# Two blocks on one core: the top-k of the gathered tokens' half first, gathers begun in the routing stage, and the output copies placed behind the last weighted sum

## The chip, the cores and the metric

The kernel runs on one core of one Trainium2 chip. The time is device microseconds of one execution of the whole program; the median of three runs is compared. The names of the engines are those of the profile: PE is TensorE (PEld its weight loads), DVE is VectorE, ACT is ScalarE, POOL is GpSimd, SP is SyncE, whose queue issues most transfers.

## What is computed

Two transformer blocks follow each other on 256 tokens of width 1024. The first mixes three branches (convolution, differential attention, attention to a memory), the second a stick-breaking attention and a recurrence. The change touches only the last part, a feed-forward stage that retrieves single neurons ("experts") by product keys:

```python
def peer_ffn(x, w_query, sub_keys, expert_u, expert_v):
    def chunk(xc):                                   # 128 tokens
        q = jnp.einsum('td,dhk->thk', xc, w_query)   # 8 heads
        q = q.reshape(TOKEN_CHUNK, PEER_HEADS, 2, PEER_HALF)
        s = jnp.einsum('thpk,hpnk->thpn', q, sub_keys)
        top_s, top_i = lax.top_k(s, PEER_TOPK)       # 16 of 128, twice per head
        cand_s = top_s[:, :, 0, :, None] + top_s[:, :, 1, None, :]
        cand_i = top_i[:, :, 0, :, None] * PEER_N_KEYS + top_i[:, :, 1, None, :]
        ...
        best_s, best_pos = lax.top_k(cand_s, PEER_TOPK)   # 16 of 256
        idx = jnp.take_along_axis(cand_i, best_pos, axis=-1)
        g = jax.nn.softmax(best_s, axis=-1)
        u = jnp.take(expert_u, idx, axis=0)          # 16384 experts
        v = jnp.take(expert_v, idx, axis=0)
        act = jax.nn.gelu(jnp.einsum('td,thkd->thk', xc, u))
        return jnp.einsum('thk,thkd->td', (g * act).astype(v.dtype), v)
```

Each token uses 8 heads x 16 = 128 experts.

## The kernel before

The first 160 tokens (`D`) are done densely: all 16384 experts are streamed. `u_pair(i)`, i = 0 to 63, multiplies two weight tiles `w` of 128x1024 (512 KB each) with the tokens and ACT applies the GELU (line 1158) into `ga`; `v_pair(i)` multiplies two tiles of `v` with `ga` and sums into four banks of PSUM, `yT` (line 1169). Between them, `ga` is multiplied by the gates, which are zero for experts that were not chosen: `onehot_group`, called 40 times (20 groups of 8 tokens, two blocks of experts each), builds one-hot matrices on DVE (`toks`, lines 1127 to 1133), multiplies them on PE (line 1136) and multiplies `ga` by the result on DVE (`mul`, line 1147).

The last 96 tokens (`NG`, all in token half t = 1) are done by gathering: for each of 96 index columns `fetch` (line 1178) fetches 128 rows of `u` from HBM into a tile `gat` (512 KB, issued by POOL), `dot` (line 1185) forms the products on DVE, `weights` applies GELU and gate, and then 96 gathers of rows of `v` are summed on DVE by `axpy` (lines 1201 and 1203) into `acc`. `rows_out` folds `acc` over partitions with a matmul (line 1231), ACT copies the result and POOL issues the output transfer (line 1234). Three buffers (`NB`) take gathers until the top-k tiles are freed; then five more (`MORE`) are there.

Ahead of both stands the routing. For each of 8 heads PE makes the query (lines 307 to 309) and the scores (line 1072); `top16` finds 16 of 128 on DVE in a first round (lines 982, 983) and a second (987 to 989); `cands` adds the two lists on POOL (line 998) and takes 16 of 256 with the same five DVE operations. `decode` turns positions into expert numbers `IDX` (lines 1015 to 1030), `gates` does the softmax and transposes `IDX` and gates on PE (lines 1053 to 1055); `rows_index` packs the index of the gathered tokens into `pk` (line 1084) and sends it by six small transfers into `gi` (line 1088), which the gathers read.

All of that waits in a list `bg` and is taken from it a few estimated microseconds at a time between the matmuls (`background(n)`). The final order on each engine is set by a scheduler that plays the program through on modelled times; each engine then works strictly in that order. `tc.issue_after(x)` tells it to put an instruction behind `x`. The steps of the gathers are paced by

```python
            def advance(i):
                box.setdefault("i0", i - 1)
                while box["n"] < (2 * NG + 1) * (i - box["i0"]) / (LAST - box["i0"]):
                    next(steps)
                    box["n"] += 1
```

with i counting the 128 pairs, so that they are spread evenly from the first call to pair 124.

Of the kernel before, what the change touches and what calls it, by code (L numbers as in the profile page):

```python
# [9 lines left out]
F32 = mybir.dt.float32  # L10
# [5 lines left out]
ALU = mybir.AluOpType  # L16
# [3 lines left out]
P = 128  # L20
# [4 lines left out]
D = T - NG  # L25
# [163 lines left out]
def build(tc, xT, memT, vec, con, con0, wcat, rgw, keysT, u, v, urow, vrow, out):  # L189
    nc = tc.nc  # L190
    es = ExitStack()
    with es:
# [26 lines left out]
        state = dict(next=0, hold=())  # L219
# [48 lines left out]
        bg = []  # L268

        def background(n, pin=False, keep=0):  # L270

            with ExitStack() as s:
                if pin:
                    s.enter_context(tc.issue_after(state["sub"].ins))
                while len(bg) > keep and n > 0:
                    c, f = bg.pop(0)
                    n -= c
                    f()
# [3 lines left out]
        def linP(x):  # L282

            ws = block()
            ps = lin_ps[0].tile([P, 2, T], F32, name="lin")[:, :, :x.shape[-1]]
            for a in range(2):
                for c in range(NC):
                    nc.tensor.matmul(ps[:, a], ws[a][:, c * P:(c + 1) * P], x[:, c], start=c == 0, stop=c == 7)  # L288
            ahead()
            return ps  # L290
# [68 lines left out]
        def statp():  # L359
            return cur["ps"].tile([P, 512], F32, name="stat", tag="stat", bufs=1)  # L360

        def attp():
            return cur["ps"].tile([P, 512], F32, name="att", tag="att", bufs=cur.get("natt", 2))
# [4 lines left out]
        def smt(n, w=512, bufs=2, dt=F32):  # L368
            return cur["sm"].tile([P, w], dt, name=n, tag=n, bufs=bufs)
# [94 lines left out]
        with ExitStack() as e1:  # L464
# [6 lines left out]
            def bigt(n, dt=F32):  # L471
# [4 lines left out]
                name=nc.get_next_instruction_name(), act_func_set_id=LN_EXP, ins=[], outs=[]))  # L476
# [125 lines left out]
            for j in range(4):  # L602
# [3 lines left out]
                g = smt("gate", 512, 3).rearrange("p (a b) -> p a b", a=2)  # L606
# [86 lines left out]
            s1, s2 = statp(), attp()  # L693
# [13 lines left out]
            for c in range(NC):  # L707
                t = smt("nrm", T)
# [70 lines left out]
            for j in range(2):  # L779
                ps = linT(h2)  # L780
                nc.vector.tensor_mul(xp[:, 2 * j:2 * j + 2, 3:], ps, bc2(rx))
                for c in (2 * j, 2 * j + 1):
                    nc.vector.tensor_scalar(xc[:, c], xp[:, c, 0:T], V("conv_w_2", c * 4), V("conv_b_2", c),
                                            op0=ALU.mult, op1=ALU.add)
# [135 lines left out]
            for j in range(2):  # L920
                for k, ps in enumerate(linK(mx, 0, None if j else (scp(), scp()))):
                    sl = slice(4 * j + 2 * k, 4 * j + 2 * k + 2)
                    g = smt("gate", 512, 3).rearrange("p (a b) -> p a b", a=2)
# [20 lines left out]
        yT = [yps.tile([P, 2, T], F32, name=f"y{b}") for b in range(4)]  # L944
# [6 lines left out]
        gi = rows.tile([P, 2, NG], F32, name="gi")  # L951
        sG = rows.tile([P, NG], F32, name="sG")
        cG = rows.tile([P, NG], F32, name="cG")
# [5 lines left out]
        with ExitStack() as e3:  # L959
# [5 lines left out]
            tk = e3.enter_context(tc.tile_pool(name="tk", bufs=1, side="right", reuse_waits="tile"))  # L965
# [5 lines left out]
            V16 = tk.tile([P, 2, 8, 2, 16], F32, name="V16")  # L971
            I16 = tk.tile([P, 2, 8, 2, 16], U32, name="I16")
# [5 lines left out]
            def top16(val, idx, src, tag):  # L978
                w = src.shape[-1]

                def f1():
                    nc.vector.max(out=val[:, 0:8], in_=src)
                    nc.vector.max_index(out=idx[:, 0:8], in_max=val[:, 0:8], in_values=src)

                def f2():
                    s2 = tk.tile([P, w], F32, name=tag, tag=tag, bufs=1)
                    nc.vector.match_replace(out=s2, in_to_replace=val[:, 0:8], in_values=src, imm_value=-3.0e38)
                    nc.vector.max(out=val[:, 8:16], in_=s2)
                    nc.vector.max_index(out=idx[:, 8:16], in_max=val[:, 8:16], in_values=s2)  # L989

                c = 0.07 + 0.00104 * w
                bg.append((2 * c, f1))
                bg.append((3 * c, f2))

            def cands(hd, t):
                def f():
                    cs = tk.tile([P, 16, 16], F32, name="cs", bufs=2)
                    nc.gpsimd.tensor_add(cs, V16[:, t, hd, 0].unsqueeze(2).to_broadcast([P, 16, 16]),
                                         V16[:, t, hd, 1].unsqueeze(1).to_broadcast([P, 16, 16]))
                    n = len(bg)  # L1000
                    top16(BS[:, t, hd], BP[:, t, hd], cs.rearrange("p a b -> p (a b)"), "cs2")
                    new = bg[n:]
                    del bg[n:]
                    bg[0:0] = new
                return f
# [27 lines left out]
            box = {}  # L1033

            def logits(t):
                def f():
                    gg_ = (pk[:, 1] if t else tk.tile([P, P], F32, name="gexp", bufs=1)).rearrange(
                        "p (a b) -> p a b", a=8)
                    nc.vector.tensor_sub(gg_, BS[:, t], BS[:, t, :, 0:1].to_broadcast([P, 8, 16]))
                    box[t] = gg_  # L1040
                return f

            def gates(t):
# [18 lines left out]
                    state["dve"] = nc.vector.tensor_copy(gT[:, 1, tl], r0)  # L1062
                return f

            for hd in range(8):
                pq = linT(h3, hd == 0)
                q = tk.tile([P, 2, T], F32, name="q", bufs=1)
                nc.scalar.copy(q, pq)
                pss = gps.tile([P, 512], F32, name="gp", tag="gp").rearrange("p (t h n) -> p t h n", t=2, h=2)
                for t in range(2):  # L1070
                    for p_ in range(2):
                        nc.tensor.matmul(pss[:, t, p_], q[:, p_, t * P:(t + 1) * P], kT[:, 2 * hd + p_],
                                         start=True, stop=True)
                ss = tk.tile([P, 2, 2, P], F32, name="ss", bufs=2)
                nc.scalar.copy(ss, pss)
                for t in range(2):
                    for p_ in range(2):
                        top16(V16[:, t, hd, p_], I16[:, t, hd, p_], ss[:, t, p_], "s2")
                    bg.append((0.0, cands(hd, t)))
                background(2.5)  # L1080
            def rows_index():


                nc.vector.scalar_tensor_tensor(pk[:, 0].bitcast(U32), IDX[:, 1, 0], float(P), IDX[:, 1, 1],
                                               op0=ALU.mult, op1=ALU.add)
                for o_, g, nq in groups:
                    for q_ in range(nq):
                        nc.gpsimd.dma_start(gi[q_ * g:(q_ + 1) * g, :, o_:o_ + g],
                                            pk[P - NG + o_:P - NG + o_ + g, :, q_ * g:(q_ + 1) * g])
# [15 lines left out]

            bg.append((0.1, rows_h))
            for t in (1, 0):
                bg.append((0.1, logits(t)))
                for q_ in range(2):
                    bg.append((4.3, decode(t, q_)))  # L1110
                bg.append((3.0, gates(t)))
                if t:
                    bg.append((0.3, rows_index))
# [39 lines left out]
            def act_of(i):  # L1153
                j = 2 * i
                return ga[0][:, j:j + 2] if j < 64 else ga[1][:, j - 64:j - 62] if j < 96 else ga[2][:, j - 96:j - 94]

            def u_pair(i):
                state["act"] = nc.scalar.activation(act_of(i), linP(h3f[:, :, :D]), AF.Gelu_apprx_tanh)  # L1158
# [38 lines left out]
            def axpy(k, m, g):  # L1197
                with tc.issue_after(state["dve"].ins):
                    if m not in acc:
                        acc[m] = rows.tile([P, 1024], F32, name=f"acc{m}", tag=f"row{m}")  # L1200
                        nc.vector.tensor_scalar_mul(acc[m], g, cG[:, k:k + 1])
                    else:
                        nc.vector.scalar_tensor_tensor(acc[m], g, cG[:, k:k + 1], acc[m], op0=ALU.mult, op1=ALU.add)  # L1203

            def gathered():

# [29 lines left out]
            acc = {}  # L1236
# [4 lines left out]
# [6 lines that stand above are left out]

            i = 0
            while bg:
                u_pair(i)  # L1250
                background(4.6)
                i += 1
# [27 lines left out]
        for b in range(4):  # L1280
            o = ga[0][:, 2 * b:2 * b + 2]
            nc.scalar.copy(o[:, 0], yT[b][:, 0, :D])  # L1282
            nc.vector.tensor_copy(o[:, 1], yT[b][:, 1, :D])  # L1283
            nc.sync.dma_start(yo[:, 2 * b:2 * b + 2], o)


# [20 lines left out]
```

## Time and profile before

| | before |
|---|---|
| median of 3 runs | 1322.68 us (1321.14 to 1325.76) |
| profiled execution, its own time | 1325.82 us |
| its span in the trace | 1324.0 us |
| PE busy | 1250.4 us (94%) |
| DVE busy | 937.6 us (71%) |
| POOL busy | 218.3 us (16%) |
| moved by DMA | 340.75 MB, mean 257 GB/s |
| weight tiles `w` of u and v, 512 KB each | 256 |
| gathers `gat`, 512 KB each | 192 |

Busy times overlap between engines. All rows below are of the profiled execution, with times counted from the start of its span.

### The profile page before, as it was taken

What the parts mean: (1) busy time and instruction counts of PE and PEld (TensorE: products, weight loads), DVE (VectorE), ACT (ScalarE), POOL (GpSimd) and SP (SyncE); (2) the same over time, 40 slices, a digit from 0 to 9 for tenths busy, and PEclk for the clock granted to TensorE, in tenths of its full rate; (3) what the DMA queues carried; (4) which work ended last, traced back from release to release, by engine and by line L of the source; (5) the groups of instructions that cost most, each with busy time, mean ns of one, the idle gap of its engine ahead of it and who ended that gap; (6) DMA issues with size and microseconds to landing.
All of it is one profiled execution on the core that took longest, in us unless ns stands there. A gap on an engine that the chain in (4) does not pass through costs nothing.

```text
span 1324.0 us, 24472 instructions
## 1 busy us (share of the span) xinstructions
PE 1250.4 (94%) x9948; PEld 1211.4 (91%) x9948; DVE 937.6 (71%) x1806; ACT 456.7 (34%) x733; POOL 218.3 (16%) x222
## 2 busy tenths in 40 slices
PE   8999999999999999998999999999999999999902
PEld 7999999899999999887999999999999999999901
DVE  6799888888997687847998544875547865440095
ACT  7546677668647458845313010000100000000000
POOL 0000000000000000000012532323412253330072
PEclk9999999999999999999999999999999999999955
DMA  8555543444565564324676999999999999999384
GB/s 293 191 191 178 164 133 120 131 139 156 161 194 174 177 203 137 124 75 157 207 260 205 410 409 408 409 388 384 379 339 353 366 384 409 409 409 409 142 334 189
DMA packets 94864, 340.75 MB, mean 257 GB/s; under 512 B 10576, under 2 KB 12048, under 8 KB 94624
## 3 DMA queue, kind: packets, MB, share of 16 engines
q1 hardware_dynamic: 66752, 237.98, 50.8%
q0 software_dynamic: 28000, 101.22, 19.9%
q8 instruction: 78, 1.28, 0.4%
q14 instruction: 34, 0.28, 0.1%
HBM read 338.01 MB, written 1.05 MB: 256 GB/s over the span
## 4 chain that ended last, share of the span: by engine, by line
PE 78%; DMA 6%; DVE 6%; issue 5%; ACT 3%; POOL 1%; POOLq 0%; SPq 0%; ACTq 0%
PE lin L288 18%; PE y L1169 15%; PE lin L308 10%; PE lin L307 10%; PE lin L309 10%; DMA w<-in_v 6%; PE gp L1136 1%; PE lin L341 1%; PE lin L343 1%; PE lin L342 1%; POOL gat L1178 1%; PE stat L459 1%; ACT whi L247 1%; DVE I L989 1%; PE sc L840 1%
## 5 line engine op out<-in xcount | busy, mean ns | idle before, releaser
L288 PE MATMUL lin<-h3f,w 128*128 128x160 f32 x2048 | 290.6, 302 | 1.8 <-issue 1.8
L1169 PE MATMUL y<-ga,w 128*128 128x160 f32 x2048 | 287.3, 301 | 1.0 <-issue 0.5
L288 PEld LDWEIGHTS lin<-h3f,w 128*128 128x128 f32 x2048 | 281.3, 191 | 3.0 <-issue 2.8
L1169 PEld LDWEIGHTS y<-ga,w 128*128 128x128 f32 x2048 | 279.4, 190 | 3.5 <-issue 1.8
L248 DVE TENSOR_TENSOR wlo<-raw,whi 128x1024 fp32r<-128x1024 f32 x188 | 229.4, 1223 | 64.3 <-ACT whi L247 63.4
L247 ACT CAST whi<-raw 128x1024 fp32r<-128x1024 f32 x188 | 196.2, 1049 | 167.7 <-PE lin L308 124.9
L308 PE MATMUL lin<-hl,whi 128*128 128x256 f32 x704 | 200.4, 285 | 0.0
L309 PE MATMUL lin<-hh,wlo 128*128 128x256 f32 x704 | 200.0, 284 | 0.0
L307 PE MATMUL lin<-hh,whi 128*128 128x256 f32 x704 | 199.9, 284 | 0.0
L1203 DVE SCALAR_TENSOR_TENSOR acc<-gat,cG,acc 128x1024 f32<-128x1024 f32 x94 | 120.8, 1285 | 55.7 <-DMA gat<-in_vrow,gi 54.1
L1185 DVE CUSTOM_DVE_ANT_0 gat<-gat,hrow 128x1024 f32<-128x1024 f32 x96 | 116.1, 1223 | 33.0 <-DMA gat<-in_urow,gi 32.9
L1178 POOL DMA_INDIRECT gat<-in_urow,gi x96 | 105.3, 1097 | 200.1 <-DVE sG L1185 187.4
L309 PEld LDWEIGHTS lin<-hh,wlo 128*128 128x128 f32 x704 | 132.7, 189 | 2.2 <-issue 1.9
L308 PEld LDWEIGHTS lin<-hl,whi 128*128 128x128 f32 x704 | 132.8, 189 | 1.7 <-issue 1.4
L307 PEld LDWEIGHTS lin<-hh,whi 128*128 128x128 f32 x704 | 132.6, 188 | 1.4 <-issue 1.0
L1178 POOL DMA_INDIRECT gat<-in_vrow,gi x96 | 96.9, 1009 | 181.2 <-DVE acc L1203 71.4
L1158 ACT ACTIVATE ga<-lin 128x320 f32<-128x320 f32 x64 | 28.0, 437 | 243.6 <-PE lin L288 230.5
L535 DVE SCALAR_TENSOR_TENSOR cacc<-ub,VT,cacc 128x256 f32<-128x256 f32 x240 | 103.9, 479 | 0.0
L955 POOL DMA_DIRECT2D fold<-in_con x1 | 0.7, 701 | 595.9 <-DVE gate L924 595.9
L1147 DVE SCALAR_TENSOR_TENSOR ga<-gp,ga 128x256 f32<-128x256 f32 (+1 forms) x60 | 29.1, 511 | 79.3 <-PE gp L1136 54.9
L1282 ACT COPY ga<-y 128x160 f32<-128x160 f32 x4 | 1.2, 292 | 206.9 <-PE y L1169 206.9
L1283 DVE COPY ga<-y 128x160 f32<-128x160 f32 x4 | 1.2, 320 | 68.7 <-ACT ga L1282 68.7
(372 smaller groups left out, 2135.2 us busy)
## 6 DMA issues: line engine op xcount, KB each, us to landing
raw<-in_wcat SPq DMA_DIRECT2D x188, 512.0 KB
w<-in_u SPq DMA_DIRECT2D x128, 512.0 KB
w<-in_v SPq DMA_DIRECT2D x128, 512.0 KB
gat<-in_urow,gi POOLq DMA_INDIRECT x96
gat<-in_vrow,gi POOLq DMA_INDIRECT x96
m_t<-in_memT SPq DMA_DIRECT2D x4, 256.0 KB
xr<-in_xT SPq DMA_DIRECT2D x2, 512.0 KB
kT<-in_keysT SPq DMA_DIRECT2D x1, 1024.0 KB
```

The costliest lines, as they stand in the source:

```text
L247: nc.scalar.copy(h, raw)
L248: state["sub"] = nc.vector.tensor_sub(l, raw, h.bitcast(F32))
L288: nc.tensor.matmul(ps[:, a], ws[a][:, c * P:(c + 1) * P], x[:, c], start=c == 0, stop=c == 7)
L307: nc.tensor.matmul(ps[:, a], wh, ah[:, c], start=(a, c) in first, stop=False)
L308: nc.tensor.matmul(ps[:, a], wh, al[:, c], start=False, stop=False)
L309: nc.tensor.matmul(ps[:, a], wl, ah[:, c], start=False, stop=(a, c) in last)
L535: nc.vector.scalar_tensor_tensor(cacc[:, c], s, w, cacc[:, c], op0=ALU.mult, op1=ALU.add)
L1147: state["dve"] = nc.vector.scalar_tensor_tensor(g_[:, :, tl], p_, 1.0 / GSCALE, g_[:, :, tl], op0=ALU.mult, op1=ALU.mult)
L1169: nc.tensor.matmul(yT[c // 2][:, c % 2, :D], ws[a][:, c * P:(c + 1) * P], g[:, a], start=False, stop=i == 63 and (a, c % 2) == (1, 1))
L1178: nc.gpsimd.indirect_dma_start(g, None, src, bass.IndirectOffsetOnAxis(gi[:, 0, k:k + 1].bitcast(U32), 0))
L1185: nc.vector.tensor_tensor_reduce(out=g, in0=g, in1=h, scale=1.0, scalar=0.0, op0=ALU.mult, op1=ALU.add, accum_out=sG[:, k:k + 1])
L1203: nc.vector.scalar_tensor_tensor(acc[m], g, cG[:, k:k + 1], acc[m], op0=ALU.mult, op1=ALU.add)
```

## The change

Three edits. First, in the loop over heads, the scores of half t = 0 go into a tile `ss0` that keeps all eight heads; only the top-k steps of half t = 1 are put into the list there, and those of t = 0 follow behind the index of the gathered tokens. Second, `rows_index` sets a mark, and from then on the loop of u pairs that works off the routing list calls `advance`, so that gathers may begin there, with the three buffers there are at that time. Third, the DVE copies of `yT` to the output tile are put behind the last `axpy` (`state["sum"]`).

```diff
@@ -1062,6 +1062,7 @@
+            ss0 = tk.tile([P, 8, 2, P], F32, name="ss0")
             for hd in range(8):
                 pq = linT(h3, hd == 0)
                 q = tk.tile([P, 2, T], F32, name="q", bufs=1)
@@ -1071,18 +1072,20 @@
-                ss = tk.tile([P, 2, 2, P], F32, name="ss", bufs=2)
-                nc.scalar.copy(ss, pss)
-                for t in range(2):
-                    for p_ in range(2):
-                        top16(V16[:, t, hd, p_], I16[:, t, hd, p_], ss[:, t, p_], "s2")
-                    bg.append((0.0, cands(hd, t)))
-                background(2.5)
+                ss = tk.tile([P, 2, P], F32, name="ss", bufs=2)
+                nc.scalar.copy(ss, pss[:, 1])
+                nc.scalar.copy(ss0[:, hd], pss[:, 0])
+                for p_ in range(2):
+                    top16(V16[:, 1, hd, p_], I16[:, 1, hd, p_], ss[:, p_], "s2")
+                bg.append((0.0, cands(hd, 1)))
+                background(3.4)
+
             def rows_index():
                 nc.vector.scalar_tensor_tensor(pk[:, 0].bitcast(U32), IDX[:, 1, 0], float(P), IDX[:, 1, 1],
                                                op0=ALU.mult, op1=ALU.add)
+                box["gi"] = True
@@ -1105,6 +1108,11 @@
             for t in (1, 0):
+                if t == 0:
+                    for hd in range(8):
+                        for p_ in range(2):
+                            top16(V16[:, 0, hd, p_], I16[:, 0, hd, p_], ss0[:, hd, p_], "s2")
+                        bg.append((0.0, cands(hd, 0)))
                 bg.append((0.1, logits(t)))
@@ -1200,7 +1208,7 @@
-                        nc.vector.scalar_tensor_tensor(acc[m], g, cG[:, k:k + 1], acc[m], op0=ALU.mult, op1=ALU.add)
+                        state["sum"] = nc.vector.scalar_tensor_tensor(acc[m], g, cG[:, k:k + 1], acc[m], op0=ALU.mult, op1=ALU.add)
@@ -1247,6 +1255,8 @@
             while bg:
+                if "gi" in box:
+                    advance(i)
                 u_pair(i)
                 background(4.6)
@@ -1280,7 +1290,8 @@
             nc.scalar.copy(o[:, 0], yT[b][:, 0, :D])
-            nc.vector.tensor_copy(o[:, 1], yT[b][:, 1, :D])
+            with tc.issue_after(state["sum"].ins):
+                nc.vector.tensor_copy(o[:, 1], yT[b][:, 1, :D])
             nc.sync.dma_start(yo[:, 2 * b:2 * b + 2], o)
```

Where the instructions stand now is shown at three places. The first is the end of DVE's program (`acc<-gat` are the weighted sums of gathered rows, `ga<-y` the copies of the dense output). Before:

```order
L1203 SCALAR_TENSOR_TENSOR acc_11562<-gat_11789,cG,acc_11562 128x1024
L1203 SCALAR_TENSOR_TENSOR acc_11562<-gat,cG,acc_11562 128x1024
L1283 COPY ga_7132<-y_7134 128x160
L1203 SCALAR_TENSOR_TENSOR acc_11562<-gat,cG,acc_11562 128x1024
L1283 COPY ga_7132<-y_7135 128x160
L1203 SCALAR_TENSOR_TENSOR acc_11562<-gat,cG,acc_11562 128x1024
L1283 COPY ga_7132<-y_7136 128x160
L1283 COPY ga_7132<-y_7137 128x160
```

And of the changed kernel, the last rows of DVE's program:

```order
L1211 SCALAR_TENSOR_TENSOR acc_11511<-gat_12329,cG,acc_11511 128x1024
L1211 SCALAR_TENSOR_TENSOR acc_11511<-gat_12352,cG,acc_11511 128x1024
L1211 SCALAR_TENSOR_TENSOR acc_11511<-gat_12375,cG,acc_11511 128x1024
L1211 SCALAR_TENSOR_TENSOR acc_11511<-gat_12378,cG,acc_11511 128x1024
L1294 COPY ga_7132<-y_7134 128x160
L1294 COPY ga_7132<-y_7135 128x160
L1294 COPY ga_7132<-y_7136 128x160
L1294 COPY ga_7132<-y_7137 128x160
```

Before, the first copy had 39 weighted sums behind it; now all four copies follow the last sum.

The second place is POOL's program at the start of the gathers (`cs` are the candidate sums of one head and token half, `gi<-pk` the index transfers, `gat<-in_urow` the gathers). Before:

```order
L998 TENSOR_TENSOR cs<-V_7191 128x256 x16
L1088 DMA gi<-pk 32x2x32 x4
L1088 DMA gi<-pk 64x2x64 x2
L1178 DMA gat<-in_urow,gi 128x1024 x3
L1178 DMA gat_8491<-in_urow,gi 128x1024
```

And in the changed kernel:

```order
L998 TENSOR_TENSOR cs<-V_7191 128x256 x11
L1091 DMA gi<-pk 32x2x32 x4
L1091 DMA gi<-pk 64x2x64 x2
L998 TENSOR_TENSOR cs<-V_7191 128x256 x2
L1186 DMA gat<-in_urow,gi 128x1024 x3
L998 TENSOR_TENSOR cs<-V_7191 128x256 x2
L1186 DMA gat<-in_urow,gi 128x1024 x3
L998 TENSOR_TENSOR cs<-V_7191 128x256
L1186 DMA gat<-in_urow,gi 128x1024 x5
```

The index transfers moved ahead of five of the sixteen candidate sums, and the gathers stand between the last of these.

The third place is DVE's program at the first two dots (ISA rows with `gat`) of the changed kernel; before, no dot stood ahead of the last top-k or decode instruction.

```order
L982 MAX BS<-cs 128x8
L988 MAX V_7191<-s_8318 128x8
L1193 ISA gat,sG<-gat,hrow_7936 128x1024
L1193 ISA sG 128x1
L983 MAX_INDEX BP<-BS,cs 128x8
L987 MATCH_REPLACE cs_8306<-BS,cs 128x256
L989 MAX_INDEX I_7192<-V_7191,s_8318 128x8
L982 MAX BS<-cs 128x8
L1193 ISA gat,sG<-gat,hrow_7936 128x1024
L1193 ISA sG 128x1
```

Eight dots now stand ahead of the end of the decode of t = 0. Of the gathers' 192 dots and sums, 99 stood ahead of the last `mul` of the one-hot groups on DVE, and 104 do now. On PE the transposes of `gates(1)` moved from u pairs 9.9 and 10.9 to 4.4 and 5.9, those of `gates(0)` from 12.2 and 13.3 to 13.4 and 14.7; the matmuls of the one-hot groups keep their places to within 1.5 pairs.

## Rows read from the trace of the kernel before

**Rows 1.** The page: DVE's busy tenths and the transfers, 40 slices of the span.

```profile
DVE  6799888888997687847998544875547865440095
...
GB/s 293 191 191 178 164 133 120 131 139 156 161 194 174 177 203 137 124 75 157 207 260 205 410 409 408 409 388 384 379 339 353 366 384 409 409 409 409 142 334 189
```

**Rows 2.** Stages: length, PE, PEld, DVE, ACT, POOL busy (count), PE clock, DMA share, GB/s.

```profile
662.00:742.00 80.00, 77.06 (x556) 75.79 (x555) 72.46 (x289) 17.96 (x31) 22.96 (x29) 0.98 0.77 263
742.00:1064.00 322.00, 322.00 (x2828) 318.79 (x2827) 202.82 (x401) 22.28 (x55) 102.23 (x95) 1.00 0.99 382
1064.00:1190.00 126.00, 125.47 (x919) 123.60 (x916) 69.59 (x56) 0.00 (x0) 53.00 (x54) 1.00 1.02 406
1190.00:1235.00 45.00, 44.56 (x320) 43.29 (x319) 0.00 (x0) 0.00 (x0) 0.72 (x1) 1.00 1.03 409
1235.00:1258.00 23.00, 23.00 (x172) 23.00 (x171) 0.00 (x0) 0.12 (x1) 0.00 (x0) 1.00 0.06 21
1258.00:1311.00 53.00, 6.41 (x34) 5.61 (x34) 50.86 (x43) 2.10 (x6) 33.34 (x32) 0.59 0.84 322
```

**Rows 3.** Timeline of the end: start, duration, instruction, count, idle before it and its releaser.

```profile
1187.22 0.95 POOL L1178 DMA_INDIRECT gat<-in_vrow,gi  x1 [1.62 <-DVE acc L1203]
1188.22 1.28 DVE L1203 SCALAR_TENSOR_TENSOR acc<-gat,cG,acc 128x1024 f32<-128x1024 f32 x1 [1.26 <-DMA gat<-in_vrow,gi]
1189.77 0.94 POOL L1178 DMA_INDIRECT gat<-in_vrow,gi  x1 [1.60 <-DVE acc L1203]
...
1258.20 0.33 DVE L1283 COPY ga<-y 128x160 f32<-128x160 f32 x1 [68.70 <-ACT ga L1282]
...
1258.56 3.74 SPq L1284 DMA_DIRECT2D out<-ga  x4
...
1259.99 1.98 POOL L1178 DMA_INDIRECT gat<-in_vrow,gi  x1 [69.28 <-DVE ga L1283]
...
1261.53 48.82 DVE L1203 SCALAR_TENSOR_TENSOR acc<-gat,cG,acc 128x1024 f32<-128x1024 f32 x37
...
1310.41 3.68 PE L1231 MATMUL lin<-acc,fold 128*64 128x512 f32 x4 [5.11 <-DVE acc L1203]
```

**Rows 4.** Transfers, 1100 to 1190 us: queue (q0 gathers, q1 weight tiles), packets, MB, share.

```profile
q0 software_dynamic: 5043, 18.36, 51.2%
q1 hardware_dynamic: 5044, 18.34, 51.1%
```

**Rows 5.** The same of 1190 to 1235 us.

```profile
q1 hardware_dynamic: 4076, 14.85, 82.7%
q0 software_dynamic: 972, 3.51, 19.7%
```

**Rows 6.** The same of 1262 to 1306 us, with the mean rate.

```profile
DMA packets 5049, 16.71 MB, mean 380 GB/s; under 512 B 540, under 2 KB 1052, under 8 KB 5048
...
q0 software_dynamic: 4504, 16.37, 95.9%
```

**Rows 7.** Transfers from 1300 to 1324 us, GB/s in slices of 0.6 us.

```profile
GB/s 403 403 410 416 410 403 416 416 403 205 27 0 0 0 0 0 0 0 0 0 0 0 0 0 0 0 55 205 178 0 0 0 0 0 0 0 0 0 0 0
```

**Rows 8.** Timeline: index transfers, the first gather, the first dot.

```profile
715.06 3.35 POOL L1088 DMA_DIRECT2D gi<-pk  x6 [13.04 <-DVE pk L1084]
...
721.77 1.84 POOL L1178 DMA_INDIRECT gat<-in_urow,gi  x1 [3.36 <-DMA gi<-pk]
...
730.20 1.26 DVE L1185 CUSTOM_DVE_ANT_0 gat<-gat,hrow 128x1024 f32<-128x1024 f32 x1 [3.11 <-DMA gat<-in_urow,gi]
```

**Rows 9.** DVE groups, 620 to 735 us: count, busy us, mean ns, idle before.

```profile
L988 DVE MAX8 V<-s 128x8 f32<-128x128 f32 x32 | 8.8, 276 | 0.0
...
L988 DVE MAX8 BS<-cs 128x8 f32<-128x256 f32 x16 | 6.5, 409 | 0.0
```

**Rows 10.** Timeline of the u pairs: PE at the first transpose, PE after the first gathers.

```profile
709.72 0.30 PE L1053 MATMUL gp<-ident,IDX 128*128 128x128 f32 x1 [1.14 <-DVE IDX L1030]
...
735.22 0.57 PEld L288 LDWEIGHTS lin<-h3f,w 128*128 128x128 f32 x4 [0.79 <-issue]
...
738.21 0.44 ACT L1158 ACTIVATE ga<-lin 128x320 f32<-128x320 f32 x1 [9.17 <-remote]
```

**Rows 11.** Timeline of ACT: two u pairs after each other at full pace.

```profile
746.17 0.44 ACT L1158 ACTIVATE ga<-lin 128x320 f32<-128x320 f32 x1 [4.06 <-PE lin L288]
750.52 0.44 ACT L1158 ACTIVATE ga<-lin 128x320 f32<-128x320 f32 x1 [3.91 <-PE lin L288]
```

## The prediction

> **What bounds the kernel now.** I read the page's slices first [rows 1]: up to slice 21 the transfers stay below 300 GB/s, from slice 22 (728 us) they run near 409 GB/s, and in slices 36 to 38 (1191 to 1291 us) DVE falls to nothing and then to 9 and transfers drop to 142 GB/s. Next the stages [rows 2]. From 742 to 1258 us PE is busy without a break at a granted clock of 1.00, so PE sets the pace there; a u pair takes 4.35 us [rows 11], a weight tile half of that, 2.17 us. Transfers run at 382 to 409 GB/s at the same time: there are two limits close together. From 1235 to 1258 us they do almost nothing (21 GB/s), and after 1258 us PE has only 6.41 us of work in 53 while DVE is full: the kernel ends with a tail of gathers alone.
>
> The timeline of the end says why [rows 3]. DVE does a weighted sum at 1188.22 and then sits idle for 68.70 us in front of the copy of `yT`, which needs PE's last matmul. With DVE, the buffers stop: POOL waits 69.28 us before its next gather at 1259.99. So 39 weighted sums and 31 gathers come after PE is done. The reader is to see that this idle time is on no engine's account but that of the order: the sums behind the copy did not need it.
>
> **Output copies behind the last sum.** This removes no work; it lets the gathers run on beside PE's last 70 us. From 1190 us on the trace has these transfers left: 14.85 MB of weight tiles and 3.51 MB of gathers already issued [rows 5], and 16.37 MB of gathers later [rows 6], 34.7 MB in all. At the 409 GB/s that stages with both queues full hold [rows 2, 4] they take 84.9 us, to 1275; in the trace the last gather's bytes landed at 1306 [rows 7]. Gain 31.1 us. If the mixed end ran only at the 380 GB/s of the gathers alone [rows 6], it would be 91.4 us and 24.6. More than 31 it can't be, since 409 is the highest rate any stage shows.
>
> Beside this I check PE. In 1100 to 1190 us both queues moved the same, 18.3 MB each [rows 4], one tile and one gather (0.524 MB each) per 2.56 us, as the gathers at 1187.22 and 1189.77 show [rows 3]. PE wants a tile per 2.17 us and lives off its ring of 13 tiles. The 28.3 tiles left at 1190 (14.85 / 0.524) then land at 1190 + 72.5 = 1262.5 instead of 1235, and PE ends some 4 us after the last, at about 1267 instead of 1258. That costs 9 us of PE and nothing at the end, because the gathers end later.
>
> Last byte to end stays: 1324.0 - 1306 = 18.0 us for the buffered sums, the fold on PE at 1310.41, ACT's copies and the output transfer [rows 3, 7]. New in it are the four copies (0.33 us each, [rows 3]) behind the last sum and SP's four output transfers (3.74 us to issue): about 5 us and their landing, beside the 13.6 us from the last sum (1310.4) to the end. So they cost nothing; without that cover they would cost their 5 us. Nothing else waits behind these copies on DVE.
>
> Here the Trainium skill speaks against the change: "DMA: Bandwidth & Descriptors", section Where 436 GB/s comes from, says that transfers from HBM are bound by about 358 GB/s per core. By that the 34.7 MB would take 97 us and end at 1287, a gain of 19 instead of 31. The trace decides otherwise: 409 GB/s over 45 us [rows 2, 5], so the Trainium skill's limit does not hold in this run.
>
> **Top-k of t = 1 first, gathers in the routing stage.** The index leaves DVE at about 714.6 us: POOL's index transfers start at 715.06 and the first gather at 721.77, waiting for them [rows 8]. In the new order ten second rounds of t = 0 and six of its 256-wide top-16 have moved behind the index: 10 x 3 x 0.276 + 6 x 5 x 0.409 = 20.6 us [rows 9]. They overlap a little, so I take 20: index at 694.5, first gather at about 701.5. The two candidate sums now ahead of it on POOL wait for DVE rows some 6 us behind the index, no longer than the index transfers take (721.77 - 715.06 = 6.7).
>
> What that is worth is not 20 us. With three buffers, and the first dot 14 us behind the index on DVE (eight second rounds and sixteen 256-wide operations, 13.2 us by [rows 9], and a microsecond of gates), gathers trickle. What survives is read from the order: 104 instead of 99 dots and sums stand ahead of the last one-hot `mul`. Between the first one-hot group and that `mul`, gathers are locked to PE's pace through DVE's order, so the lead stays 5 gathers: 2.62 MB or 6.4 us at 409 GB/s. Bounds: 0, if DVE or POOL lose it again; 8 gathers (10 us), if the stage after 1064 us starts with three more already landed.
>
> Eight second copies on ACT (half of the old copy each) cost ACT's start-up only; ACT is busy 17.96 us of 80 there [rows 2]. Nothing is on the path.
>
> **What the early gathers cost PE.** PE works in order, and the transposes of `gates` wait for DVE. Before, PE waited 1.14 us at the first one [rows 10]. It now meets that transpose 5.5 pairs earlier: 708.6 - 5.5 x 4.35 = 684.7 us. DVE's first decode, counted in the same way some 8 us ahead of the index, ends at 686.5: 2 us. The transposes of `gates(0)` come 7.5 pairs after the second of `gates(1)` (694 us), at 727. DVE was through with both halves at 730.20 - 3.11 = 727.1 [rows 8], the first decode of t = 0 some 5 us before. Now seven dots stand ahead of that decode (7 x 1.22 = 8.5 us), and they wait for gathers: the first landed 8.4 us after its issue [rows 8], so at 710, about 3 us after DVE gets there. That gives 722 + 8.5 + 3 = 734 and a wait of 7 us on PE, between 2 (the rows just fit) and 12 (each dot waits). I add 2 us for a lower clock behind so long a gap. Against it, the first eight gathers at once cost PE 9.17 - 4.0 = 5.2 us at 738.21 [rows 10, 11], with three buffers perhaps nothing. Net: 2 + 7 + 2 - 1.1 - 5.2 = +4.7; I take +5, from -5 (no waits) to +15 (long waits, and a burst when five buffers come later). This moves everything behind it, since PE has no idle time to give up until 1258 [rows 2].
>
> **The sum.** Last gather byte: 1306 - 31.1 - 6.4 + 5 = 1273.5; plus 18.0 gives a span of 1291.5, 32.5 us less. The profiled execution's own time is 1325.82, so it would be 1293.3; the median of the runs is 1322.68, and I predict **1290 us**. All low bounds together (31.1 + 10 + 5) give 1277, all high ones (24.6 + 0 - 15) 1313.
>
> **Rivals.** *PE becomes the end.* If the lead is larger and PE loses nothing, gathers end with the weight tiles and the end is PE's: 1267 minus a few us, plus 14 for sums, fold and output: span 1280, **1279 us**. For: PE is unbroken to 1258. Against: the order keeps the lead at 5. Chance 0.16.
>
> *The early start is lost in the routing stage.* DVE's dots wait in order, `gates(0)` comes late, PE stands 12 us or more, or the burst recurs: the first part turns into a loss of 5 to 12 us against a gain of 31. Span 1298 to 1305, **1300 us**. For: three buffers, eight dots ahead of the decode. Against: first landing 8.4 us is short beside the 14 us DVE needs from index to first dot. Chance 0.22.
>
> *The mixed rate does not hold.* With all gathers in flight to the end, transfers fall to the 380 GB/s of [rows 6]: 6.5 us later, 1296 us, and 1303 with no lead. Against: [rows 2, 4, 5]. Chance 0.04. By the limit of the Trainium skill named above, the same sum would give 1301 us.
>
> *Slower than before.* While gathers take half of the transfers, PE is short of tiles from about 1207 us. Should its clock fall to the lower level (1.2 GHz), a tile takes 4.35 instead of 2.56 us, 1.8 us more each; with some 23 tiles left then, PE ends 41 us later, at 1313, and the kernel near **1322**. It decides from 24 tiles on: if the clock falls before 1205 us and stays low, the change loses. Clocks below 1 stand in stages where PE had gaps of microseconds (0.98 in 662 to 742, 0.59 after 1258, [rows 2]); from 1064 to 1190, short gaps for tiles included, it stayed 1.00. The Trainium skill ("TensorE: Matmul & The Clock Gate", section HAM oscillation — how this bites in real kernels) describes such a fall in kernels that wait for data after every few matmuls; no stage here shows it at gaps this short. Chance 0.03.
>
> *No change* would need the order to be without effect; the copies do stand last on DVE. Chance 0.01.
>
> **How the numbers follow.** My forecast, 1284 to 1297 us, holds 0.54. The range reaches to the first two rivals, 1279 to 1302, and leaves out the ends of both, the poor rate's worst and the slow clock: about 2 in 10. A measurement of this kernel can tell 0.3%, 4 us. Faster 0.96, the same 0.02 (no change, and half of the slow-clock rival), slower 0.02.
>
> **What would show it.** Right: no idle of DVE over a few us after 1064 us; transfers at 409 GB/s up to the last gather, at 1268 to 1280; PE's last matmul between 1260 and 1273, with a few tenths of waiting per tile after about 1210; first gather at 701 us; PE waiting at the transpose of `gates(0)` near 727 us. Wrong: a first gather near 721, DVE waits of over 10 us for gathers ahead of t = 0's decode, a clock below 1 between 1200 and 1260, or a gap of over 20 us between the last tile and the last gather.

## The result and the profile after

The changed kernel takes 1291.35 us (median of 3 runs, 1290.32 to 1291.59) where the kernel before takes 1322.68: a ratio of 0.9757, 95% interval 0.9728 to 0.9786. It is faster by 31.3 us. Its profiled execution has a span of 1289.6 us, 34.4 us under that of before, whose profiled execution was itself 3.1 us above its median (1325.82 us).

The page: the same two rows as in [rows 1], 40 slices of a span that is now 1289.6 us.

```profile
DVE  6889988888998777855899864588545886445444
...
GB/s 294 189 194 182 164 138 124 132 116 147 164 200 161 196 202 157 148 67 99 181 235 240 354 409 409 409 408 363 382 383 342 356 360 392 409 409 408 409 409 231
```

DVE no longer falls to 0 and rises to 9 at the end; it keeps a 4 or 5 up to the last slice, and the transfers stay at 408 to 409 GB/s where [rows 1] has the 142.

The stages, in the columns of [rows 2] (the last three in place of its last one, since the end has moved):

```profile
662.00:742.00 80.00, 74.29 (x539) 73.33 (x538) 73.72 (x290) 16.95 (x29) 26.50 (x33) 0.98 0.82 285
742.00:1064.00 322.00, 322.00 (x2817) 318.76 (x2816) 207.50 (x408) 22.39 (x55) 101.07 (x96) 1.00 0.99 382
1064.00:1190.00 126.00, 126.00 (x930) 124.26 (x929) 67.66 (x55) 0.00 (x0) 51.87 (x53) 1.00 1.02 404
1190.00:1235.00 45.00, 43.03 (x292) 39.82 (x291) 21.86 (x18) 0.00 (x0) 16.10 (x17) 1.00 1.03 409
1235.00:1258.00 23.00, 21.05 (x140) 18.88 (x138) 11.55 (x10) 0.00 (x0) 8.52 (x9) 1.00 1.03 409
1258.00:1276.00 18.00, 15.39 (x103) 13.94 (x104) 11.48 (x10) 2.12 (x6) 2.86 (x4) 1.00 0.86 341
1276.00:1290.00 14.00, 3.15 (x16) 1.44 (x13) 2.55 (x6) 1.16 (x2) 1.12 (x2) 0.73 0.29 75
```

From 1190 to 1258 us DVE now works (21.86 and 11.55 us, against 0.00 before), and PE is no longer full: 43.03 of 45 and 21.05 of 23 us. Its clock stays at 1.00 to 1276 us.

The transfers of 1190 to 1235 us, as in [rows 5]:

```profile
DMA packets 5043, 18.39 MB, mean 409 GB/s; under 512 B 560, under 2 KB 560, under 8 KB 5040
...
q1 hardware_dynamic: 2520, 9.18, 51.2%
q0 software_dynamic: 2520, 9.18, 51.0%
```

Both queues move the same 9.18 MB; before, the weight tiles had 14.85 MB of it.

The timeline of the end, which answers to [rows 3]:

```profile
1263.65 0.95 POOL L1186 DMA_INDIRECT gat<-in_vrow,gi  x1 [1.62 <-DVE acc L1211]
1264.65 1.28 DVE L1211 SCALAR_TENSOR_TENSOR acc<-gat,cG,acc 128x1024 f32<-128x1024 f32 x1 [1.27 <-DMA gat<-in_vrow,gi]
1265.73 2.20 PEld L1177 LDWEIGHTS y<-ga,w 128*128 128x128 f32 x16 [0.36 <-DMA w<-in_v]
...
1269.77 7.89 DVE L1211 SCALAR_TENSOR_TENSOR acc<-gat,cG,acc 128x1024 f32<-128x1024 f32 x6 [1.28 <-DMA gat<-in_vrow,gi]
...
1270.83 3.53 PE L1177 MATMUL y<-ga,w 128*128 128x160 f32 x24 [1.18 <-DMA w<-in_v]
...
1277.58 1.01 DVE L1294 COPY ga<-y 128x160 f32<-128x160 f32 x4
...
1277.71 1.93 PE L1239 MATMUL lin<-acc,fold 128*64 128x512 f32 x4 [0.50 <-DVE acc L1211]
1277.92 2.00 SPq L1295 DMA_DIRECT2D out<-ga  x4
...
1280.55 0.58 POOL L1242 DMA_DIRECT2D out<-gat  x1 [4.02 <-ACT gat L1241]
```

The 68.70 us of idle time on DVE and the 69.28 us on POOL [rows 3] are gone. In their place stand waits of 1.27 us for a gather and 0.36 us for a weight tile (on PEld), one of each per 2.56 us. PE's last matmul of `y` ends at 1274.36 us, the last weighted sum at 1277.66, and the copies follow it in 1.01 us.

The first index, gather and dot, which answer to [rows 8]:

```profile
694.26 3.35 POOL L1091 DMA_DIRECT2D gi<-pk  x6 [0.92 <-DVE pk L1086]
...
700.79 1.05 POOL L1186 DMA_INDIRECT gat<-in_urow,gi  x1 [0.29 <-PE lin L288]
...
708.93 1.23 DVE L1193 CUSTOM_DVE_ANT_0 gat<-gat,hrow 128x1024 f32<-128x1024 f32 x1 [1.67 <-DMA gat<-in_urow,gi]
```

PE at the routing, which answers to [rows 10], and the ACT instruction that one of its waits goes back to (`gexp` are the exponentials of the softmax in `gates`):

```profile
686.41 0.33 PE L1053 MATMUL gp<-ident,IDX 128*128 128x128 f32 x1 [0.37 <-DVE IDX L1030]
...
726.39 2.17 PE L288 MATMUL lin<-h3f,w 128*128 128x160 f32 x14 [1.71 <-ACT ga L1166]
731.91 0.33 PE L1053 MATMUL gp<-ident,IDX 128*128 128x128 f32 x1 [3.35 <-DVE IDX L1030]
```

```profile
724.28 0.31 ACT L1048 ACTIVATE gexp<-gexp 128x128 f32<-128x128 f32 x1 [6.51 <-DVE gexp L1039]
```

### The profile page after: what moved, and what is told of

Same layout as the page of the kernel before. It is cut to its first block, busy times and chain, and to the rows that moved or that the text cites. A ratio compares the mean times of both kernels' runs of the same rounds, so it can differ in the third digit from the quotient of the medians.

```text
span 1289.6 us, 24478 instructions
## 1 busy us (share of the span) xinstructions
PE 1253.5 (97%) x9948; PEld 1211.0 (94%) x9948; DVE 937.0 (73%) x1806; ACT 457.3 (35%) x741; POOL 214.6 (17%) x222
## 3 DMA queue, kind: packets, MB, share of 16 engines
q8 instruction: 78, 1.28, 0.4%
## 4 chain that ended last, share of the span: by engine, by line
PE 43%; issue 20%; DMA 16%; DVE 11%; POOL 6%; ACT 3%; POOLq 0%; SPq 0%; DVEq 0%; ACTq 0%
DMA gat<-in_vrow,gi 10%; PE lin L308 10%; PE lin L307 10%; PE lin L309 10%; POOL gat L1186 6%; DMA gat<-in_urow,gi 5%; DVE acc L1211 2%; PE lin L341 1%; DVE gat L1193 1%; PE lin L343 1%; PE lin L342 1%; DVE wlo L248 1%; PE stat L459 1%; ACT whi L247 1%; DVE I L983 1%
## 5 line engine op out<-in xcount | busy, mean ns | idle before, releaser
L1177 PE MATMUL y<-ga,w 128*128 128x160 f32 x2048 | 293.0, 302 | 5.6 <-DMA w<-in_v 2.8
L1177 PEld LDWEIGHTS y<-ga,w 128*128 128x128 f32 x2048 | 279.9, 190 | 13.3 <-DMA w<-in_v 10.4
L1186 POOL DMA_INDIRECT gat<-in_vrow,gi x96 | 93.3, 972 | 162.6 <-DVE acc L1211 127.4
L308 PE MATMUL lin<-h3lo,whi 128*128 128x256 f32 x128 | 37.3, 291 | 2.3 <-DVE h3lo L384 2.3
```

What stands on the lines that cost most here:

```text
L308: nc.tensor.matmul(ps[:, a], wh, al[:, c], start=False, stop=False)
L1177: nc.tensor.matmul(yT[c // 2][:, c % 2, :D], ws[a][:, c * P:(c + 1) * P], g[:, a], start=False, stop=i == 63 and (a, c % 2) == (1, 1))
L1186: nc.gpsimd.indirect_dma_start(g, None, src, bass.IndirectOffsetOnAxis(gi[:, 0, k:k + 1].bitcast(U32), 0))
```

## The experiments

The theory after the result: nearly all of the gain comes from the four copies, and the end is bound by transfers that the two queues share evenly. The rivals: the earlier start brings a good part of it; or PE's late end has another cause than the transfers. Four kernels were timed together with the kernel before (1323.89 us, median of 15 runs), three others later, again with it (1323.36 us, 9 runs). "Lead" is the number of dots and sums that stand ahead of the last one-hot `mul` on DVE.

**Only the copies moved** (the kernel before with the third edit alone; `state["sum"]` is set as in the change):

```diff
...
-            nc.vector.tensor_copy(o[:, 1], yT[b][:, 1, :D])
+            with tc.issue_after(state["sum"].ins):
+                nc.vector.tensor_copy(o[:, 1], yT[b][:, 1, :D])
```

> The kernel before with the third edit alone (copies of yT behind the last weighted sum). Theory A (DVE's place of the copies was the whole cost, the early gathers give back about what they take): 34.7 MB left at 1190 us end at 1275 us, plus 18 us less a few for a full clock: a span of 1290 to 1294, a median of 1289 to 1294 us, within 3 us of the full change. Theory B (the gathers begun 20 us earlier carry a good part of the 31 us): 1303 to 1312 us.

Measured: 1295.27 us (1294.32 to 1298.24), ratio 0.978 (0.9763 to 0.9798), 28.6 us less; the span is 1293.4. The end of its timeline:

```profile
1264.27 3.53 PE L1169 MATMUL y<-ga,w 128*128 128x160 f32 x24 [1.19 <-DMA w<-in_v]
...
1265.30 14.49 DVE L1203 SCALAR_TENSOR_TENSOR acc<-gat,cG,acc 128x1024 f32<-128x1024 f32 x11 [0.33 <-DMA gat<-in_vrow,gi]
...
1279.84 3.67 PE L1231 MATMUL lin<-acc,fold 128*64 128x512 f32 x4 [6.68 <-DVE acc L1203]
```

So this edit alone brings 28.6 of some 31 us; its interval and that of the changed kernel overlap, so what the other two edits add is not shown by these two times. PE's last matmul of `y` ends here at 1267.80, with gathers still coming: the end is the gathers'. The last eleven sums follow each other without a wait: from 1265.30 us on DVE keeps the pace, at 1.3 us a sum.

**The copies on ACT** (the kernel before, with no wait on the sums, and the second copy of each pair moved to ACT):

```diff
-            nc.vector.tensor_copy(o[:, 1], yT[b][:, 1, :D])
+            nc.scalar.copy(o[:, 1], yT[b][:, 1, :D])
```

> The kernel before with both copies of each pair of yT on ACT, none on DVE, and nothing put behind anything. Theory A (a DVE instruction that waits for PE's last matmul held the sums queued behind it): DVE runs through, 1289 to 1295 us, like the third edit alone. Rival (the sums were held by something else that the edit's order also moved, such as the buffers or the gate values): 1318 to 1325 us.

Measured: 1297.22 us (1294.64 to 1299.78), ratio 0.979 (0.9771 to 0.981), 2 us above the range of the theory and 21 us under that of the rival. The cause of the old stall is thus that the copies stood in DVE's order, not when they were done or where their output went. The 2 us are not traced to one cause: in its trace the dense output's transfers run beside the last gathers, and the last five sums wait 0.18 to 0.19 us each for theirs, where the copies alone have no wait.

**Only the early start** (the first two edits, the copies as before):

```diff
-            with tc.issue_after(state["sum"].ins):
-                nc.vector.tensor_copy(o[:, 1], yT[b][:, 1, :D])
+            nc.vector.tensor_copy(o[:, 1], yT[b][:, 1, :D])
```

> The changed kernel without the third edit: top-k order and early gathers alone; the copies then have 35 weighted sums behind them instead of 39. Theory A: DVE stands about 60 us in front of the copy again, four gathers fewer in the tail (4 x 1.32 = 5.3 us), PE's end 4 us later: 1318 to 1323 us. Theory B: 1300 to 1310 us.

Measured: 1321.9 us (11 runs, 1318.41 to 1323.47), ratio 0.9976 (0.9965 to 0.9987): 2 us less. The end of its timeline:

```profile
1260.49 0.32 DVE L1293 COPY ga<-y 128x160 f32<-128x160 f32 x1 [66.98 <-ACT ga L1292]
...
1262.27 1.98 POOL L1186 DMA_INDIRECT gat<-in_vrow,gi  x1 [67.56 <-DVE ga L1293]
```

The stall is nearly as long as before (66.98 against 68.70 us) and ends 2.3 us later, since PE ends later. By the written order 35 instead of 39 sums stand behind the first copy, 4 x 1.3 = 5 us; less the 2.3 us this is the 3.0 us between the two spans (1321.0 and 1324.0). Without the third edit the early start is worth hardly anything.

**The new order without early gathers** (the changed kernel, `advance` not called beside the routing list):

```diff
-                if "gi" in box:
-                    advance(i)
```

> The changed kernel without the call of advance in the loop of u pairs: t = 1 first and the copies last, but gathers begin after the routing as before (101 instead of 104 dots and sums ahead of the last one-hot product). Theory A: PE no longer waits about 3.4 us at the transpose of gates(0) near 728 us, since no dot stands ahead of the decode, and three gathers of lead are lost (3.8 us of transfers): 1289 to 1294 us, the same as the full change to 3 us. Theory B: 1300 us or more.

Measured: 1290.82 us (1290.01 to 1293.93), ratio 0.9742 (0.9726 to 0.9757). That is no worse than the changed kernel, and 4.5 us under the copies alone, which were timed together with it. Three rows of its trace (of the longest of its runs) say why, POOL and PE:

```profile
701.74 1.04 POOL L1186 DMA_INDIRECT gat<-in_urow,gi  x1 [0.30 <-PE lin L288]
...
718.65 3.53 PE L288 MATMUL lin<-h3f,w 128*128 128x160 f32 x24 [1.72 <-ACT ga L1166]
...
1278.22 3.67 PE L1239 MATMUL lin<-acc,fold 128*64 128x512 f32 x4 [6.68 <-DVE acc L1211]
```

The first three gathers, as many as there are buffers, still go out early, at 701.74 us, because the index is early; only their dots stay behind the decode of t = 0. So DVE isn't held by gathers there, and PE has no wait at `gates(0)` (only the 1.72 us behind ACT). The last one-hot `mul` on DVE, which ends the stage in which gathers follow PE, shows the trade (first row this kernel, second the changed one; the copies alone have theirs at 1063.56):

```profile
1063.67 0.76 DVE L1155 SCALAR_TENSOR_TENSOR ga<-gp,ga 128x256 f32<-128x256 f32 x2 [1.65 <-PE gp L1144]
```

```profile
1068.04 0.75 DVE L1155 SCALAR_TENSOR_TENSOR ga<-gp,ga 128x256 f32<-128x256 f32 x2 [3.05 <-PE gp L1144]
```

By the written order, 101 dots and sums stand ahead of it here, 104 in the changed kernel, 99 before. The early dots buy three gathers (3 x 1.28 = 3.8 us of transfers) for 4.4 us of PE. Counted from the first transpose, where this execution was 0.94 us behind the other (687.35 against 686.41), it is 5.3 us: the 3.35 us of waiting at `gates(0)` and the lower clock behind it. Nothing is left. The two gathers that this kernel has ahead of the copies alone cost no such price. They are worth 2.6 us of transfers; the two spans differ by 1.6 us and the medians by 4.5, so what else is in the medians stays open.

**Twenty gathers less** (the changed kernel; the last 20 of the 96 `v` gathers and their weighted sums are left out):

```diff
-                        for k in range(o_, o_ + g):
+                        for k in range(o_, o_ + g - 20 * (f is axpy and m == 1)):
...
-                    next(steps)
+                    next(steps, None)
```

> This kernel leaves out the last 20 of the 96 gathers of v rows and their weighted sums (the other orders stay). Theory: the end of the changed kernel is bound by transfers that two queues share evenly, and PE waits there only because its weight tiles get half of them. Without the 20 gathers (10.5 MB, 25.6 us at 409 GB/s) the last gather lands about 51 us earlier, near 1222 us, and from then on the weight tiles have all of the transfers: PE's last matmul of y moves from 1274 back to 1262 to 1266 us, and the span to 1272 to 1277 us. Rival: PE is held up at the end by something else than transfers (its clock, or the weighted sums of DVE beside it); then its last matmul stays at 1271 us or later, and the span at 1283 us or more.

Measured: one run, 1279.38 us, span 1277.6. Stages and timeline:

```profile
1190.00:1235.00 45.00, 42.77 (x300) 40.66 (x299) 20.73 (x17) 0.00 (x0) 8.52 (x9) 1.00 1.03 409
1235.00:1258.00 23.00, 23.00 (x171) 23.00 (x171) 0.00 (x0) 0.00 (x0) 0.00 (x0) 1.00 0.48 190
```

```profile
1227.13 37.60 PE L1177 MATMUL y<-ga,w 128*128 128x160 f32 x272 [1.40 <-DMA w<-in_v]
...
1229.77 1.28 DVE L1211 SCALAR_TENSOR_TENSOR acc<-gat,cG,acc 128x1024 f32<-128x1024 f32 x1 [1.28 <-DMA gat<-in_vrow,gi]
```

As soon as the gathers are through, PE runs without a break: 37.60 us for 272 matmuls, 23.00 of 23 us. Its last matmul of `y` ends at 1227.13 + 37.60 = 1264.7 us instead of 1274.4. Of these 9.7 us, 1.2 come from the front (its last one-hot `mul` is at 1066.83, not 1068.04); the other 8.5 us of PE's late end belong to the gathers, as the theory says. The sums went with the gathers, so this run does not tell DVE's work from the transfers; but PEld's waits are for `w<-in_v`, and from 1064 to 1190 us PE was full (126.00 of 126 us) beside 67.66 us of DVE's work. The span is 0.6 us above the range given, because 12.9 us follow PE's end.

**One more gather buffer** (`NB, MORE = 3, 6` instead of `3, 5`), without the early gathers and with them. Each time the last one-hot `mul` moves from pair 84 to 81 of the 128 on PE (what the expectations call u pairs lies among the v pairs here).

> The changed kernel without the early calls of advance, and with six instead of five extra gather buffers, so that nine gathers can be held. The last mul of the one-hot groups stands at u pair 81 instead of 84 on PE, with 102 instead of 104 dots and sums ahead of it on DVE. Theory (the lead at that mul and the transfers after it set the end): DVE is free of PE's pace some 3 x 4.35 = 13 us earlier with 2 gathers (5 us at 2.56 us each) less, so the last byte comes 2 to 4 us earlier, the time is 1286 to 1290 us. Rival: what is gained in front is lost in the routing stage or PE's last matmul near 1274 us is the end by now; then 1290 to 1295 us.

> The changed kernel with six instead of five extra gather buffers. The last mul of the one-hot groups stands at u pair 81 instead of 84, with 101 instead of 104 dots and sums ahead of it. Theory (lead and transfers): 13 us earlier with 3 gathers (7.7 us) less, so 1 to 4 us are gained: 1287 to 1291 us. Rival: a longer burst of gathers costs PE in its issue, and the end is PE's: 1291 to 1296 us.

Measured: 1289.9 us (1285.62 to 1290.97), ratio 0.9743 (0.9726 to 0.9759), and 1290.94 us (1288.93 to 1291.1), ratio 0.9748 (0.9735 to 0.9761). Both medians lie at the upper ends of the theory's ranges, where the rivals' begin, and the intervals overlap with that of the changed kernel, so the times neither establish a gain nor tell the two apart. The first one's trace says why a longer lead brings little:

```profile
1268.55 3.53 PE L1177 MATMUL y<-ga,w 128*128 128x160 f32 x24 [1.17 <-DMA w<-in_v]
1269.53 1.29 DVE L1211 SCALAR_TENSOR_TENSOR acc<-gat,cG,acc 128x1024 f32<-128x1024 f32 x1 [0.28 <-DMA gat<-in_vrow,gi]
```

The last weighted sum ends at 1270.82, PE's last matmul of `y` at 1272.08: with the longer lead PE becomes the end, in a span of 1286.8 us. Beside the run without early gathers, its last sum ends 7.3 us earlier and PE's last matmul of `y` 3.5 us later (1268.55 there).

## Why the prediction was right

Predicted were 1290 us and a span of 1291.5; measured 1291.35 and 1289.6. The copies carry the gain, as predicted. In the smaller terms errors offset each other. Point by point:

- **The copies.** 31.1 us were predicted for the last byte of the gathers (1306 to 1274.9). With this edit alone, the transfers of 1268 to 1280 us fall to half of their rate at 1275.2 us (slices of 0.3 us), the span is 30.6 us shorter, and the medians differ by 28.6:

```profile
GB/s 423 396 396 410 396 369 341 423 423 437 369 355 341 410 355 396 423 437 396 423 396 369 328 273 205 123 123 109 96 55 55 41 14 0 0 0 0 0 0 0
```

  The 409 GB/s of the mixed end hold in both stages from 1190 to 1258 us. The limit of 358 GB/s that the Trainium skill gives ("DMA: Bandwidth & Descriptors", section Where 436 GB/s comes from), by which the sum came to 1301 us, is not seen here, with one core running.
- **The lead.** Predicted were 6.4 us for five gathers, and 5 us of PE against it; the last byte at 1273.5. The first dot was at 708.93 us, 21 us earlier than before, and the first gather at 700.79 (predicted 701.5). PE's last one-hot matmul moved by 3.7 us. Beside the copies alone, the transfers fall to half 2.4 us earlier (1272.8 by the same view, below, against 1275.2), where 1.4 was predicted. The run without early gathers shows what the prediction did not separate: the two gathers of lead that the index brings cost PE nothing (its last `mul` is at 1063.67, that of the copies alone at 1063.56), and the three that early dots bring cost it 4.4 to 5.3 us. The view of the changed kernel:

```profile
GB/s 396 396 410 423 437 410 382 382 396 410 369 328 300 300 273 246 205 178 164 109 109 68 82 14 27 0 0 0 0 0 205 218 14 0 0 0 241 288 303 303
```

- **PE at the routing.** Predicted 2 us at `gates(1)`, measured 0.37 and, at its second half, 0.28. Predicted 7 us at `gates(0)` near 727 us, measured 3.35 at 731.91. The 1.71 us at 726.39 were not in the sum: ACT waits 6.51 us in order for DVE's logits before the `gexp`, and PE's `u` pairs need the gelus queued behind it. Together 5.06 us against 7, within 2 to 12. The 2 us for a lower clock were right: from 732 to 739.2 us, behind these waits, the granted clock is 0.76, which is 1.7 us of these 7.2:

```profile
732.00:739.20 7.20, 7.20 (x42) 7.20 (x43) 5.10 (x8) 0.44 (x1) 3.58 (x3) 0.76 0.75 244
```

- **The burst of gathers.** The prediction gave 5.2 us back for a stop of PE at the first eight gathers [rows 10]. It was 4.5 us: the next gelu in that trace came early (at 741.68, after 3.03 us of idle time instead of 3.91), and by 750.52 the gelus were 4.5 us behind a pace of 4.35. The kernel with the copies alone issues its gathers in the same order and shows no such stop (its gelus from 726 to 744 us come every 4.3 to 4.6 us), nor does the one with the copies on ACT. So this term was a trait of one execution; why it was there is open. Both have another wait instead, which the changed kernel and that of before lack: ACT holds its gelus for an activation that needs DVE's dots (`cG<-sG`), and PE waits 1.52 us behind it (2.60 with the copies on ACT). With the copies alone:

```profile
770.60 0.22 ACT L1194 ACTIVATE cG<-sG 128x16 f32<-128x16 f32 x1 [9.15 <-DVE sG L1185]
771.19 26.35 PE L288 MATMUL lin<-h3f,w 128*128 128x160 f32 x192 [1.52 <-ACT ga L1158]
```

- **The front in all.** Predicted +5 us; DVE's last one-hot `mul` moved by 3.7 (1064.31 to 1068.04). The rows add up to 0.65 + 1.71 + 3.35 us of waits and 1.7 us for the clock, less the 1.1 and 4.5 us of before: 1.8 us. A further 1.1 us is older than the change: this execution was that much behind already at the transfer of `fold` (597.4 against 596.3 us), ahead of the routing. The other 0.8 us are open. So 3.7 is near 5 partly by luck.
- **PE at the end.** Predicted 1267 us, or between 1260 and 1273; measured 1274.36. The 1267 left out that the front part moves PE too. With the copies alone it was 1267.80, as worked out. From there it is 6.6 us: the last one-hot `mul` is 4.5 us later, the rest is weight tiles that landed later. This is the term that was mis-sized: the prediction says that its 5 us move "everything behind" the routing, and left the 1267 where it was. It didn't count: the last sum still ended 3.3 us behind PE. The rival that PE becomes the end was closer than its 0.16 says, and a kernel with one more buffer is in it.
- **The tail.** 18.0 us predicted between the last byte and the end, some 16.8 measured; 18.2 with the copies alone. The fold on PE took 1.93 us instead of 3.67, since it ran at a granted clock of 1.00 (2.4 GHz), behind other matmuls that ended 0.50 us before, where the copies alone have 0.51 (1.2 GHz) behind 6.68 us of idle time. This gain comes of PE's late end; the prediction did not have it. The fold's stretch in the changed kernel, then with the copies alone:

```profile
1277.70:1279.60 1.90, 1.89 (x4) 0.47 (x4) 0.89 (x4) 0.58 (x1) 0.00 (x0) 1.00 0.39 116
1279.80:1283.50 3.70, 3.66 (x4) 0.74 (x4) 0.92 (x4) 0.58 (x1) 0.00 (x0) 0.51 0.59 177
```

  The four copies and SP's 2.00 us lie beside the fold, and POOL's transfer at 1280.55 ends last: they cost nothing, as predicted.
- **The slow clock** did not come: 1.00 from 1190 to 1276 us with waits of 0.36 us per tile, as the stage at 1064 us had let expect. The Trainium skill's warning ("TensorE: Matmul & The Clock Gate", section HAM oscillation — how this bites in real kernels) shows here only behind waits of microseconds (0.76 from 732 to 739 us, 0.51 in the fold of the copies alone), not at these short ones.

## What to carry to other kernels

An instruction that waits for another engine's last result belongs at the end of its queue, or on a queue where nothing waits behind it: here four copies of 0.33 us held 39 sums and 31 gathers for 69 us, and either cure was worth 27 to 29 us. A kernel that is short of transfers at its end gains from an earlier start only what the engines in between let pass: look at what follows the moved work in order (here dots ahead of a decode), and count it against the lead. And where two queues share the transfers evenly, moving gathers beside weight tiles delays the weight tiles; work out both ends, since the later one is the kernel's.

## What was not expected of the hardware

Two queues with work share the transfers to the packet: 2520 and 2520 packets, 9.18 and 9.18 MB, in 45 us, at 409 GB/s, so a ring of 13 tiles runs dry though nothing is slower. Four fold matmuls took 3.67 us after 6.68 us of idle time on PE, at a granted clock of 0.51, and 1.93 us after 0.50 us, at 1.00. And a single `exp` on ACT, 0.31 us long, held ACT for 6.51 us and by that PE for 1.71 us, in the changed kernel and, for 6.53 and 1.72 us, in the one without early gathers; before, the `gexp` at 716.98 us waited for nothing. The new order of the top-k work has made the logits of t = 0 late for it.
